# The scan's products of a pair of heads in three steps: by one direction's states, by the other's, by the inputs

## The chip, the cores and the metric

The kernel runs on one core of a Trainium2 chip, in one launch. The metric is the device time of the launch in microseconds (us). An execution under the hardware profiler gives the timelines quoted here.

## The reference

One layer of a diffusion backbone over 1024 latent tokens and 256 context tokens, width 1024: attention beside a bidirectional state-space scan, merged by gates, then a mixture of experts. The change is in the scan alone. Per direction it is a chunked recurrence:

```python
def ssd_chunked(xh, dt, a, bm, cm, h0, with_output):
    ...
    acum = jnp.cumsum(dtc * a, axis=2)
    ...
    cb = jnp.einsum('bcign,bcjgn->bcijg', cc, bc)
    y_diag = jnp.einsum('bcijg,bcijgr,bcjgr,bcjgrp->bcigrp', cb, decay, dtc, xc)
    y_off = jnp.einsum('bcign,cbgrpn,bcigr->bcigrp', cc, h_prev, jnp.exp(acum))
    y = (y_diag + y_off).reshape(nb, nl, ng, nr, npd)
```

There are 16 heads of 64 columns in 4 groups (a group shares B and C, of 128 states each). The output of a chunk is a sum of three products: the inputs of the chunk by a decayed matrix C B^T (`y_diag`, both directions in one matrix here), and C with the decay, by the forward state and by the backward state that come into the chunk (`y_off`, twice).

## The kernel before, in words

All of the layer's mixers run as coroutines of one planner, the class `Flow`. Each coroutine yields what it needs next: tiles, a free buffer of a ring, an engine, a time. The planner keeps a modelled clock for each engine and a modelled ready time for each tile. It resumes the coroutine that it thinks can go first, by priority, and the instructions are written into the engines' queues in that order. So the order on each engine is fixed when the program is built, and changing what a coroutine waits for can move instructions elsewhere. On the chip each engine runs its own queue in order, and semaphores hold an instruction until its operands are there.

The stage that matters is `mixer_t`. A server coroutine (the lowest priority) runs the in-projection: 24 multiplies of 512 columns for each bank (`acc`, four banks of PSUM; `hi`, `lo` are the split weights, `hh`, `hl` the split input). Its results go to the convolution (`conv_post`: ACT writes `ux`, `uB` or `uC` from the bank, then DVE adds two shifted copies per bank, after which the bank is free), or to gates. When the four convolutions of a group are there, `group` starts: it transposes the inputs (`xn`) and B (`Bn`), starts `states` once per direction (`hp[0]`, `hp[1]`: the states that enter each of the eight chunks of 128 tokens), multiplies C by B (`CB`, through the banks `aux`), and goes through four blocks: two pairs of heads by two halves of four chunks.

For each block and head, `unit` makes the operands. Two loads bring the cumulated decays, `R[0]` and `R[1]` (SP's queue, six buffers). DVE writes `W` by eight steps from the step sizes. POOL subtracts a column from `R[0]` into `G`, DVE's four steps combine it with `R[1]`, ACT takes the exponential. POOL multiplies W by CB, and DVE multiplies W by G: the matrix for the inputs. In `decays`, ACT takes the exponential of each R and POOL multiplies it by C: the matrices for the states. There are two buffers each of `W` and `G`.

`products` then runs 24 products of 128 columns into one bank `py`: for each of the four chunks W by xn, R[0] by hp[0], R[1] by hp[1], each for both heads, which take the two halves of the bank's partitions. It waits until both heads are listed in `ready`, and until 400 ns past the modelled ready times of their W and R. Afterwards the buffers go back, and `evac` adds the skip term and the gate on DVE. After four blocks `norm` ends the group.

Lines: L148 is every matmul, L156 activations, L171 and L175 two-tensor operations on DVE and POOL, L180 and L187 DVE operations with a column.

Of the kernel before, what the change touches and what calls it, by code (L numbers as in the profile page):

```python
# [19 lines left out]
P = 128  # L20
# [54 lines left out]
def _n(ap):  # L75
    return ap.tensor.name
# [299 lines left out]
class Layer:  # L376
# [413 lines left out]
    def mixer_t(s):  # L790
        tc, nc, I, F = s.tc, s.nc, s.I, s.F
# [9 lines left out]
        if True:  # L801
            acc = s.ring(pp, [P, 512], "acc", 4)
            aux = s.ring(pq, [P, 512], "aux", 2)
            pys = s.ring(pq, [P, 512], "py", 2)
# [11 lines left out]
            Rs = s.ring(sp, [P, 512], "R", 6)  # L816
            Gs = s.ring(sp, [P, 4, P], "G", 2)
            Ws = s.ring(sp, [P, 4, P], "W", 2)
# [172 lines left out]
            def group(g, x0, x1, B, C):  # L991
                x = (x0, x1)
                yield [lambda: state["dt"], xns, Bns]
                xn, Bn = xns.get(), Bns.get()
# [10 lines left out]
                for c in range(0, 10, 4):  # L1005
                    n = min(4, 10 - c)
# [8 lines left out]
                hp = [q.get() for q in hps]  # L1015
                done, left = [], [16]
# [4 lines left out]
                for half in range(2):  # L1021
                    yield [C, B, aux]
                    pt = aux.get()
                    for i in range(4):
                        c = 2 + half * 4 + i
# [6 lines left out]
                for pair in range(2):  # L1032
                    for half in range(2):
                        yield [pys]
                        py, ready = pys.get(), []
                        for hh in range(2):
                            yield [(Rs, 2), "NOW"]
                            F.spawn(0, unit(g, pair, half, hh, CB, C, ready))
                        F.spawn(1, products(g, pair, half, xn, hp, py, done, ready, yt))
# [39 lines left out]
            def unit(g, pair, half, hh, CB, C, ready):  # L1079

                r = 2 * pair + hh
                h = 4 * g + r
                t0 = 512 * half
                R = [Rs.get(), Rs.get()]
                for d in range(2):
                    F.dma(R[d], bass.AP(tensor=s.acd[d].tensor, offset=s.acd[d].offset + h * T + t0, ap=[[0, P], [1, 512]]))
                Rv = [q.rearrange("p (c i) -> p c i", i=P) for q in R]
                yield [Gs, Ws, "DVE"]
                G, W = Gs.get(), Ws.get()
                cs = range(4 * half, 4 * half + 4)  # L1090
                for c in range(4):
                    F.ts(W[:, c], s.le, dt[:, 2 + cs[c], h:h + 1], None, ALU.mult)
                for c in range(4):
                    F.stt(W[:, c], s.ge, dt[:, 2 + cs[c], 16 + h:16 + h + 1], W[:, c], ALU.mult, ALU.add)
                yield [R[0], "POOL"]
                F.ptt(G, Rv[0], ac[:, 0, 2 + 4 * half:6 + 4 * half, h:h + 1].to_broadcast([P, 4, P]), ALU.subtract)
                yield [G, R[1], "DVE"]
                for c in range(4):
                    F.stt(G[:, c], Rv[1][:, c], ac[:, 1, 2 + cs[c], h:h + 1], G[:, c], ALU.subtract, ALU.min)
                k = []  # L1100
                F.spawn(0, decays(R, C[:, t0:t0 + 512], k, F.clk["DVE"] + 100.0))
                yield [CB, W, "POOL"]
                F.ptt(W, W, CB[:, 4 * half:4 * half + 4], ALU.mult)
                yield [G, "ACT"]
                F.act(G, G, AF.Exp)
                yield [G, "DVE"]
                F.tt(W, W, G, ALU.mult)
                Gs.put(G)
                yield [lambda: len(k) == 2]
                ready.append((hh, W, *R))  # L1110

            def products(g, pair, half, xn, hp, py, done, ready, yt):

                yield [lambda: len(done) == 2 and len(ready) == 2]
                yield [hp[0], hp[1], *(F.ready[_n(q)] + 400.0 for v in ready for q in v[1:])]
                for c in range(4):
                    n = 4 * half + c
                    for i, src in enumerate((xn[:, 2 + n], hp[0][:, n], hp[1][:, n])):
                        for v in ready:
                            o = 64 * v[0]  # L1120
                            x = 128 * pair + o
                            F.mm(py[o:o + 64, c * P:(c + 1) * P], src[:, x:x + 64], v[1 + i].rearrange("p c i -> p (c i)")[:, c * P:(c + 1) * P] if i == 0 else v[1 + i][:, c * P:(c + 1) * P], i == 0, i == 2, 134.5)
                for _, W, R0, R1 in ready:
                    Rs.put(R0, R1)
                    Ws.put(W)
                yield from evac(g, pair, half, py, yt)

            def decays(R, C, k, at):
                for q in R:
                    yield [q, at, "ACT"]  # L1130
                    F.act(q, q, AF.Exp)
                    yield [q, "POOL"]
                    F.ptt(q, q, C, ALU.mult)
                    k.append(1)

            def evac(g, pair, half, py, yt):
                sl = slice(512 * half, 512 * half + 512)
# [1346 lines left out]
```

## Time and profile before

| what | us |
|---|---|
| median of 3 runs | 2785.7 (2785.47 to 2786.71) |
| the profiled execution | 2800.41 |
| its span | 2798.6 |
| PE busy in the span | 2618.5 |
| DVE busy in the span | 2013.0 |
| ACT, POOL busy in the span | 1340.7, 903.0 |

PE is TensorE's matmuls, DVE is VectorE, ACT is ScalarE, POOL is GpSimd, SP the queue that issues loads. A timeline row has the start, the duration, the engine, the line, the operation, out<-in, partitions by elements, and a count where equal instructions stand in sequence. Brackets at its end hold the idle time of the engine just before it, and what ended it. Durations of matmuls overlap: the distance of two starts tells what one costs. The scan's blocks run from about 500 to 1005 us; the four groups follow one another. A waits row counts idle time of one engine by what released it.

### The profile page before, as it was taken

The page shows a single profiled execution, that of the slowest core. Times are in us where ns is not written, and L with a number is a line of the kernel's source. Part 1 is how long each engine was busy: PE and PEld are TensorE (multiplying, and loading weights), DVE is VectorE, ACT ScalarE, POOL GpSimd, SP SyncE. Part 2 cuts the span into 40 slices and gives each one's busy share as a digit, 9 for nine tenths or more (in the row PEclk, how much of TensorE's full clock was granted, in tenths as well). Part 3 has the DMA queues.
Part 4 walks back from the last instruction along what each step waited for, and adds up shares of the span by engine and source line. Part 5 has one row for each costly group of instructions (what it writes and reads, how often), then busy time and mean ns, then how long its engine had stood idle before and what let it go on. Part 6 is the DMA issues. An engine that isn't in the chain of part 4 may idle for free.

```text
span 2798.6 us, 41131 instructions
## 1 busy us (share of the span) xinstructions
PE 2618.5 (94%) x14561; PEld 2101.1 (75%) x14561; DVE 2013.0 (72%) x4680; ACT 1340.7 (48%) x2104; POOL 903.0 (32%) x669
## 2 busy tenths in 40 slices
PE   7999999999999999999999999889999999999991
PEld 4888878778788777888887687668887776777660
DVE  6877133768686749888894767867788877788863
ACT  4211123344443546666664422435666656676651
POOL 0111010545353520000000000055656656677841
PEclk9999999999999999999999999999999999999996
DMA  7767253242334354223233953568899998999997
GB/s 277 224 206 216 64 143 105 67 139 91 121 91 132 106 172 145 82 91 141 93 102 125 292 179 133 188 216 264 276 309 297 315 299 278 307 321 328 314 316 233
DMA packets 275409, 545.67 MB, mean 195 GB/s; under 512 B 31562, under 2 KB 166835, under 8 KB 248194
## 3 DMA queue, kind: packets, MB, share of 16 engines
q1 hardware_dynamic: 239330, 437.14, 45.6%
q0 software_dynamic: 35872, 105.88, 14.8%
q8 instruction: 115, 1.88, 0.3%
q14 instruction: 92, 0.75, 0.1%
HBM read 433.78 MB, written 124.73 MB: 200 GB/s over the span
## 4 chain that ended last, share of the span: by engine, by line
PE 58%; DMA 10%; DVE 9%; issue 4%; ACT 2%; POOL 2%; SPq 0%; POOLq 0%; ACTq 0%; DVEq 0%
PE gu L148 16%; PE acc L148 10%; PE dn L148 9%; PE bacc L148 5%; PE sps L148 5%; PE pv L148 4%; DMA cr<-cumd,crow 3%; PE xt L152 2%; PE tr L152 2%; PE aux L148 2%; DVE G L187 2%; DMA qk<-qk 2%; DMA braw<-in_w_branch_attn_dram 1%; DVE gl L171 1%; DVE W L180 1%
## 5 line engine op out<-in xcount | busy, mean ns | idle before, releaser
L171 DVE TENSOR_TENSOR gl<-raw,gh 128x1024 fp32r<-128x1024 f32 x240 | 288.2, 1218 | 35.4 <-ACT gh L164 33.7
L148 PE MATMUL acc<-hh,hi 128*128 128x512 f32 (+2 forms) x760 | 304.7, 401 | 1.3 <-DVE ux L187 1.3
L148 PE MATMUL acc<-hl,hi 128*128 128x512 f32 (+2 forms) x760 | 289.3, 381 | 0.0
L164 ACT CAST gh<-raw 128x1024 fp32r<-128x1024 f32 x240 | 246.6, 1050 | 88.0 <-PE gu L148 59.2
L148 PE MATMUL acc<-hh,lo 128*128 128x512 f32 (+1 forms) x736 | 280.9, 382 | 2.5 <-DVE lo L171 2.5
L148 PE MATMUL gu<-gh,xh 128*128 128x512 f32 (+3 forms) x672 | 278.4, 414 | 0.6 <-ACT gh L164 0.6
L148 PE MATMUL gu<-gl,xh 128*128 128x512 f32 (+3 forms) x672 | 264.5, 394 | 6.2 <-DVE gl L171 4.4
L148 PE MATMUL gu<-gh,xl 128*128 128x512 f32 (+3 forms) x672 | 264.5, 394 | 0.0
L193 DVE TENSOR_SCALAR_CACHE_REDUCE e<-sps 128x512 f32<-128x512 f32 (+1 forms) x384 | 214.4, 597 | 32.9 <-PE sps L148 32.6
L262 POOL DMA_INDIRECT cr<-cumd,crow x98 | 123.4, 1260 | 316.1 <-DMA wtab<-sc 281.2
L268 POOL DMA_INDIRECT yacc<-y,tk x98 | 181.3, 1850 | 96.8 <-issue 23.2
L148 PE MATMUL sps<-qk 128*128 128x512 f32 (+1 forms) x768 | 195.6, 386 | 9.3 <-DMA qk<-qk 5.1
L156 ACT ACTIVATE e<-e,st 128x1280 f32<-128x1280 f32 x128 | 174.7, 1366 | 32.0 <-DVE st L202 31.8
L262 POOL DMA_INDIRECT wc<-wtab,tk x98 | 148.6, 1516 | 121.0 <-DVE tk L182 85.9
L148 PE MATMUL acc<-hi,hh 128*128 128x512 f32 x448 | 181.3, 405 | 0.0
L148 PE MATMUL acc<-hi,hl 128*128 128x512 f32 x448 | 176.2, 393 | 0.4 <-DVE hl L171 0.4
L148 PE MATMUL acc<-lo,hh 128*128 128x512 f32 x448 | 176.0, 393 | 0.0
L148 PEld LDWEIGHTS sps<-qk 128*128 128x128 f32 x768 | 141.2, 192 | 41.3 <-DVE e L193 8.3
L148 PEld LDWEIGHTS acc<-hh,hi 128*128 128x128 f32 (+1 forms) x760 | 142.6, 188 | 32.9 <-issue 4.0
L148 PE MATMUL pv<-wr,vv 128*128 128x256 f32 x640 | 165.1, 381 | 0.0
L148 PEld LDWEIGHTS acc<-hl,hi 128*128 128x128 f32 (+1 forms) x760 | 142.6, 188 | 27.4 <-issue 0.8
L148 PEld LDWEIGHTS acc<-hh,lo 128*128 128x128 f32 x736 | 138.7, 188 | 32.1 <-DVE lo L171 3.3
(327 smaller groups left out, 6264.3 us busy)
## 6 DMA issues: line engine op xcount, KB each, us to landing
raw<-in_w_e_gate_dram SPq DMA_DIRECT2D x64, 1024.0 KB
raw<-in_w_e_up_dram SPq DMA_DIRECT2D x64, 1024.0 KB
draw<-in_w_e_down_dram SPq DMA_DIRECT2D x64, 1024.0 KB
qk<-qk POOLq DMA_DIRECT2D x16, 1664.0 KB
raw<-in_w_in_dram SPq DMA_DIRECT2D x40, 512.0 KB
wada<-in_w_ada_dram SPq DMA_DIRECT2D x32, 512.0 KB
R<-acd SPq DMA_DIRECT2D x64, 256.0 KB
qk<-sa SPq DMA_DIRECT2D x52, 256.0 KB
```

The costliest lines, as they stand in the source:

```text
L148: s.nc.tensor.matmul(out, l, r, start=start, stop=stop)
L152: s.nc.tensor.transpose(out, in_, ident)
L156: s.nc.scalar.activation(out, in_, fn, **kw)
L164: s.nc.scalar.copy(out, in_)
L171: s.nc.vector.tensor_tensor(out, a, b, op=op)
L180: s.nc.vector.tensor_scalar(out, a, s1, s2, op0=op0)
L187: s.nc.vector.scalar_tensor_tensor(out, a, sc, b, op0=op0, op1=op1)
L193: s.nc.vector.tensor_scalar(out, a, s1, None, op0=op0, op1=op1, accum_out=acc)
L262: s.nc.gpsimd.indirect_dma_start(out=out, out_offset=None, in_=table, in_offset=bass.IndirectOffsetOnAxis(ap=idx, axis=0), **kw)
L268: s.nc.gpsimd.indirect_dma_start(out=table, out_offset=bass.IndirectOffsetOnAxis(ap=idx, axis=0), in_=in_, in_offset=None, compute_op=ALU. ...
```

## The change

`products` makes three steps instead of one loop over chunks. First R[0] by hp[0] for all four chunks and both heads, then R[1] by hp[1], then W by xn. Each step waits for its own operands, until 600 ns past the modelled ready time in the first two steps and 1000 ns in the last. `ready` becomes two lists: `decays` adds the R of a head to the first, `unit` adds its W to the second, and no longer waits for its `decays`. The R buffers go back after the second step, the W buffers after the third. The bank's start flag is set on the first chunk of the first step only, its stop flag on the last chunk of the last.

```diff
--- before.py
+++ after.py
@@ -1032,7 +1032,7 @@
                 for pair in range(2):
                     for half in range(2):
                         yield [pys]
-                        py, ready = pys.get(), []
+                        py, ready = pys.get(), ([], [])
                         for hh in range(2):
                             yield [(Rs, 2), "NOW"]
                             F.spawn(0, unit(g, pair, half, hh, CB, C, ready))
@@ -1097,8 +1097,7 @@
                 yield [G, R[1], "DVE"]
                 for c in range(4):
                     F.stt(G[:, c], Rv[1][:, c], ac[:, 1, 2 + cs[c], h:h + 1], G[:, c], ALU.subtract, ALU.min)
-                k = []
-                F.spawn(0, decays(R, C[:, t0:t0 + 512], k, F.clk["DVE"] + 100.0))
+                F.spawn(0, decays(R, C[:, t0:t0 + 512], hh, ready[0], F.clk["DVE"] + 100.0))
                 yield [CB, W, "POOL"]
                 F.ptt(W, W, CB[:, 4 * half:4 * half + 4], ALU.mult)
                 yield [G, "ACT"]
@@ -1106,32 +1105,40 @@
                 yield [G, "DVE"]
                 F.tt(W, W, G, ALU.mult)
                 Gs.put(G)
-                yield [lambda: len(k) == 2]
-                ready.append((hh, W, *R))
+                ready[1].append((hh, W))
 
             def products(g, pair, half, xn, hp, py, done, ready, yt):
 
-                yield [lambda: len(done) == 2 and len(ready) == 2]
-                yield [hp[0], hp[1], *(F.ready[_n(q)] + 400.0 for v in ready for q in v[1:])]
-                for c in range(4):
-                    n = 4 * half + c
-                    for i, src in enumerate((xn[:, 2 + n], hp[0][:, n], hp[1][:, n])):
-                        for v in ready:
-                            o = 64 * v[0]
+                yield [lambda: len(done) == 2 and len(ready[0]) == 2]
+
+                def part(srcs, ws, first, last):
+                    for c in range(4):
+                        for hh, w in ws:
+                            o = 64 * hh
                             x = 128 * pair + o
-                            F.mm(py[o:o + 64, c * P:(c + 1) * P], src[:, x:x + 64], v[1 + i].rearrange("p c i -> p (c i)")[:, c * P:(c + 1) * P] if i == 0 else v[1 + i][:, c * P:(c + 1) * P], i == 0, i == 2, 134.5)
-                for _, W, R0, R1 in ready:
-                    Rs.put(R0, R1)
-                    Ws.put(W)
+                            F.mm(py[o:o + 64, c * P:(c + 1) * P], srcs[c][:, x:x + 64], w[:, c * P:(c + 1) * P], first and c == 0, last and c == 3, 134.5)
+
+                ns = range(4 * half, 4 * half + 4)
+                for d in range(2):
+                    ws = [(v[0], v[1 + d]) for v in ready[0]]
+                    yield [hp[d], *(F.ready[_n(w)] + 600.0 for _, w in ws)]
+                    part([hp[d][:, n] for n in ns], ws, d == 0, False)
+                for v in ready[0]:
+                    Rs.put(*v[1:])
+                yield [lambda: len(ready[1]) == 2]
+                yield [xn, *(F.ready[_n(w)] + 1000.0 for _, w in ready[1])]
+                part([xn[:, 2 + n] for n in ns], [(hh, w.rearrange("p c i -> p (c i)")) for hh, w in ready[1]], False, True)
+                for _, w in ready[1]:
+                    Ws.put(w)
                 yield from evac(g, pair, half, py, yt)
 
-            def decays(R, C, k, at):
+            def decays(R, C, hh, ready, at):
                 for q in R:
                     yield [q, at, "ACT"]
                     F.act(q, q, AF.Exp)
                     yield [q, "POOL"]
                     F.ptt(q, q, C, ALU.mult)
-                    k.append(1)
+                ready.append((hh, *R))
 
             def evac(g, pair, half, py, yt):
                 sl = slice(512 * half, 512 * half + 512)
```

Each engine has the same instructions as before but for three fewer table loads on ACT. Up to the first block, and again from the first products of the branches that follow the scan, the orders are equal. The first place is PE at the fourth block of the first group; `hp_3824` and `hp_3825` are the forward and the backward states. Before (the pattern of the last rows goes on to 24 products):

```order
L148 MATMUL acc<-hh_85,hi 128x512
L148 MATMUL acc<-hl_86,hi 128x512
L148 MATMUL acc<-hh_85,lo 128x512
L148 MATMUL py<-W,xn 64x128 x2
L148 MATMUL py<-R,hp_3824 64x128 x2
L148 MATMUL py<-R,hp_3825 64x128 x2
L148 MATMUL py<-W,xn 64x128 x2
L148 MATMUL py<-R,hp_3824 64x128 x2
L148 MATMUL py<-R,hp_3825 64x128 x2
```

Now:

```order
L148 MATMUL acc<-hh_83,lo 128x512
L148 MATMUL py<-R,hp_3824 64x128 x8
L148 MATMUL acc<-hh_83,hi 128x512
L148 MATMUL acc<-hl_84,hi 128x512
L148 MATMUL acc<-hh_83,lo 128x512
L148 MATMUL acc<-hh_83,hi 128x512
L148 MATMUL acc<-hl_84,hi 128x512
L148 MATMUL acc<-hh_83,lo 128x512
L148 MATMUL py<-R,hp_3825 64x128 x8
L148 MATMUL py<-W,xn 64x128 x8
L148 MATMUL acc<-hh_85,hi 128x512
L148 MATMUL acc<-hl_86,hi 128x512
```

The block comes after 9 fewer accumulations, and six stand between its first two steps. This is one of four such blocks; in the other twelve the steps stand back to back.

The second place is DVE at the start of the second group's blocks, where the states' last steps (hp) meet the first block's W and G. Before:

```order
L187 SCALAR_TENSOR_TENSOR hp_4988<-hp_4988,cdec,aux 128x64 x12
L187 SCALAR_TENSOR_TENSOR ux<-acc,vcol,ux 128x512
L187 SCALAR_TENSOR_TENSOR ux<-acc,vcol,ux 128x511 x2
L187 SCALAR_TENSOR_TENSOR ux<-acc,vcol,ux 128x512
L187 SCALAR_TENSOR_TENSOR ux<-acc,vcol,ux 128x255 x2
L171 TENSOR_TENSOR lo<-raw,hi 128x512
L180 TENSOR_SCALAR W<-cst,dtn 128x128 x4
L187 SCALAR_TENSOR_TENSOR W<-cst,dtn,W 128x128 x4
L180 TENSOR_SCALAR W<-cst,dtn 128x128 x4
L187 SCALAR_TENSOR_TENSOR W<-cst,dtn,W 128x128 x4
L187 SCALAR_TENSOR_TENSOR G<-R,ac,G 128x128 x8
L171 TENSOR_TENSOR W<-W,G 128x512
```

Now (the planner has given the states of the same direction the name `hp_4995`):

```order
L187 SCALAR_TENSOR_TENSOR hp_4995<-hp_4995,cdec,aux 128x64 x8
L180 TENSOR_SCALAR W<-cst,dtn 128x128 x4
L187 SCALAR_TENSOR_TENSOR W<-cst,dtn,W 128x128 x4
L187 SCALAR_TENSOR_TENSOR hp_4995<-hp_4995,cdec,aux 128x64 x4
L180 TENSOR_SCALAR W<-cst,dtn 128x128 x4
L187 SCALAR_TENSOR_TENSOR W<-cst,dtn,W 128x128 x4
L187 SCALAR_TENSOR_TENSOR hp_4995<-hp_4995,cdec,aux 128x64 x4
L187 SCALAR_TENSOR_TENSOR G<-R,ac,G 128x128 x8
L171 TENSOR_TENSOR W<-W,G 128x512
L187 SCALAR_TENSOR_TENSOR ux<-acc,vcol,ux 128x512
L171 TENSOR_TENSOR W<-W,G 128x512
L187 SCALAR_TENSOR_TENSOR ux<-acc,vcol,ux 128x511
```

Both heads' W now stand ahead of the last steps of the states, and the convolution's steps (ux) behind the first multiply of W by G. In the first group it was like this before already.

The third place is PE just ahead of the second group's first block, now, with the semaphores that an instruction waits for (`DVE_49`, `Pool_49` are counters of DVE and of POOL):

```order
L148 MATMUL acc<-hl_84,hi 128x512
L148 MATMUL acc<-hh_83,lo 128x512
L148 MATMUL acc<-hh_85,hi 128x512 [waits DVE_49]
L148 MATMUL acc<-hl_86,hi 128x512
L148 MATMUL acc<-hh_85,lo 128x512
L148 MATMUL acc<-hh_85,hi 128x512
L148 MATMUL acc<-hl_86,hi 128x512
L148 MATMUL acc<-hh_85,lo 128x512
L148 MATMUL acc<-hh_85,hi 128x512
L148 MATMUL acc<-hl_86,hi 128x512
L148 MATMUL acc<-hh_85,lo 128x512
L148 MATMUL py<-R,hp_4994 64x128 [waits Pool_49] x2
```

The accumulation into a fresh bank waits for a step of DVE, which is `ux<-acc` of the rows above; eight more and the block stand behind it. The third group has the same.

## Rows read from the trace of the kernel before

**Rows 1.** The page's first line.

```profile
span 2798.6 us, 41131 instructions
```

**Rows 2.** Busy time by engine, clock, DMA share, in two stretches of the scan.

```profile
500.00:1005.00 505.00, 479.23 (x2798) 395.92 (x2797) 370.92 (x874) 229.36 (x326) 239.67 (x198) 0.99 0.36 108
...
680.00:720.00 40.00, 36.77 (x236) 29.74 (x235) 37.98 (x67) 19.61 (x28) 25.56 (x20) 1.00 0.38 120
```

**Rows 3.** PE's waits, 500 to 1010: in total, times, longest.

```profile
PE py L148 <- DVE W L171: 14.5, 8, 2.6
...
PE py L148 <- POOL R L175: 7.3, 9, 3.3
```

**Rows 4.** The chain, 495 to 515: start, us, what.

```profile
507.93 2.09 PE acc L148 x9
```

**Rows 5.** PE's timeline, first group: start, us, instruction, [idle before it, its releaser].

```profile
521.28 0.58 PE L148 MATMUL acc<-hh,hi 128*128 128x512 f32 x1
...
532.76 0.50 PE L148 MATMUL acc<-hh,hi 128*128 128x512 f32 x1 [1.30 <-DVE ux L187]
...
535.07 0.44 PE L148 MATMUL py<-W,xn 128*64 128x128 f32 x4
...
537.84 0.50 PE L148 MATMUL acc<-hh,hi 128*128 128x512 f32 x1
...
553.34 0.32 PE L148 MATMUL py<-R,hp 128*64 128x128 f32 x1 [0.48 <-POOL R L175]
...
572.97 0.32 PE L148 MATMUL py<-R,hp 128*64 128x128 f32 x1 [0.47 <-POOL R L175]
...
591.82 0.32 PE L148 MATMUL py<-R,hp 128*64 128x128 f32 x1 [0.47 <-POOL R L175]
...
595.67 0.61 PE L148 MATMUL acc<-hh,hi 128*128 128x512 f32 x1
```

**Rows 6.** DVE's timeline, first group.

```profile
522.44 0.87 DVE L180 TENSOR_SCALAR W<-cst,dtn 128x128 f32<-128x128 f32 x4
...
524.28 2.19 DVE L187 SCALAR_TENSOR_TENSOR G<-R,ac,G 128x128 f32<-128x128 f32 x8
...
539.34 1.14 DVE L187 SCALAR_TENSOR_TENSOR G<-R,ac,G 128x128 f32<-128x128 f32 x4
...
583.85 5.27 DVE L187 SCALAR_TENSOR_TENSOR G<-R,ac,G 128x128 f32<-128x128 f32 x4 [0.95 <-POOL G L175]
```

**Rows 7.** PE's timeline, second group.

```profile
648.39 0.47 PE L148 MATMUL acc<-hh,hi 128*128 128x256 f32 x1
...
649.29 1.05 PE L148 MATMUL aux<-uC,uB 128*128 128x128 f32 x8
...
725.80 0.47 PE L148 MATMUL py<-W,xn 128*64 128x128 f32 x1 [2.64 <-DVE W L171]
...
730.13 0.50 PE L148 MATMUL acc<-hh,hi 128*128 128x512 f32 x1
```

**Rows 8.** POOL's timeline, first group.

```profile
528.50 6.38 POOL L175 TENSOR_TENSOR R<-R,uC 128x512 f32<-128x512 f32 x4 [0.88 <-ACT R L156]
...
582.49 1.33 POOL L175 TENSOR_TENSOR G<-R,ac 128x512 f32<-128x512 f32 x1 [1.91 <-DMA R<-acd]
```

**Rows 9.** PE's timeline, third group.

```profile
782.75 0.47 PE L148 MATMUL acc<-hh,hi 128*128 128x256 f32 x1
...
859.84 0.32 PE L148 MATMUL py<-W,xn 128*64 128x128 f32 x1 [0.62 <-DVE W L171]
...
862.61 0.50 PE L148 MATMUL acc<-hh,hi 128*128 128x512 f32 x1
```

**Rows 10.** Busy time and clock around the wait in the second group.

```profile
725.00:730.00 5.00, 4.20 (x46) 4.15 (x46) 2.55 (x4) 3.59 (x6) 1.46 (x2) 0.66 0.28 53
```

**Rows 11.** PE's timeline, end of the scan.

```profile
1004.92 1.05 PE L148 MATMUL aux<-cst,G 128*128 128x1 f32 x8 [0.40 <-POOL G L175]
...
1032.12 0.50 PE L148 MATMUL bacc<-bxh,bwh 128*128 128x512 f32 x1 [0.47 <-ACT bxh L164]
```

## The prediction

> **What bounds the kernel now.** I read the page's totals first, then the stretch in which the scan runs, then TensorE's waits there, then the timelines of single blocks. The profiled execution took 2800.41 us for a span of 2798.6 [rows 1]; the sum below is made against it, and since the runs shown have a median of 2785.7 (2785.47 to 2786.71), 0.53% less, the result is scaled by 2785.7 / 2800.41 = 0.99475. In the scan, 500 to 1005 us, PE is busy for 479.23 of 505 us [rows 2]: so all that any order of the products can win there is about 26 us, 0.9% of the kernel. The table of PE's waits names them: 14.5 us in 8 waits of a product for DVE's last multiply of W, 7.3 us in 9 waits for POOL's multiply of R [rows 3]. The reader is to see that these waits are not spread: between two product blocks PE has accumulations of the in-projection (0.233 us each, 9 in 2.09) [rows 4] until they run out, and then it stands. What it stands for is the chain of the next pair's operands on DVE, POOL and ACT. In 680 to 720, DVE is busy for 37.98 of 40 us [rows 2]. So the scan has two engines close to full, and a stretch is as long as the longer of them: PE's work placed there, or DVE's chain of blocks.
>
> **What the change does to PE's order.** The products stay the same 24 per block, 2.77 us from the first to the next accumulation (535.07 to 537.84) [rows 5]. Of 16 blocks, 12 have their three steps without anything between; only four have six accumulations (6 x 0.233 = 1.4 us) between the first step and the second. So the change of order inside a block moves little by itself. What it moves is where the planner puts whole blocks. From the planned order I count PE's work between the last state product and the end of the fourth block. In the second and third group it falls by 66 accumulations of 512 columns (66 x 0.233 = 15.4), six of 256 (half of that each, 0.7) and the eight products C by B (649.29 to 650.10 on PE's clock, about 0.8 for four and four beside each other, so 2 x 0.8 = 1.6) [rows 7]: 17.7 us in each of the two groups. In the first group it falls by nine accumulations, 2.1 us; in the fourth it is equal. This work does not go away: it stands before the states or after the scan, where the order now has 96 more accumulations ahead of the branches' first products. There it costs its own time. So a group gains only if its block chain gets shorter by more than the work taken out of it.
>
> **The first group, as a measure of the chain.** Its start in the new order is the same as now, and the new second and third groups are ordered like it: W of the first block is set before the last states are done. From the accumulation behind the last state product (521.28) to the end of block 1 (537.84) are 16.56 us [rows 5]. Then the last operand, each time a POOL multiply of R, came at 553.34, 572.97 and 591.82 [rows 5]: 15.50 us after the end of block 1, then 19.63 and 18.85.
>
> **The second and third group after.** *Block 1.* PE could end it 8.6 us after the anchor if nothing were late (25 accumulations, 5.8, and 2.77 for the block): the lower bound. The upper bound is the first group's 16.56. Of that, one set of W, 1.84 us (522.44 to 524.28) [rows 6], now stands ahead of the states' last steps, and POOL's idle 0.88 us before its four multiplies of R [rows 8], which was ACT's late first exponential, should go. 16.56 - 1.84 - 0.88 = 13.8. I take it, because those multiplies ended at 534.88 (528.50 + 6.38) and the products began at 535.07: the row that the block hangs on. The added wait belongs here: in the new order the nine accumulations just ahead of block 1 need a bank that DVE's convolution step (ux<-acc) empties, and that stands behind the multiply of W by G of the first head. The first group has the pattern already: 1.30 us at 532.76 [rows 5]. Behind that accumulation stand the other eight and then block 1 itself. It is inside the 13.8.
> *The steps.* R comes free after the second step, eight products (0.92 us, a third of 2.77) before the block's end. The two later blocks each had a first POOL subtraction waiting for the load of R (1.91 at 582.49) [rows 8], so I take 0.92 off the two later intervals: 18.71 and 17.93. Lower bound for an interval: 15.50, the shortest seen; upper: as before. When R lands last, the first eight products have run, and 16 remain: 1.85 us.
> *The clock.* After a wait the fourth block of the second group ran its 22 last products in 4.33 us (725.80 to 730.13) instead of 2.54, with a granted clock of 0.66 as a mean over 725 to 730 [rows 7, 10], so part of it at the lower of the two levels, 1.2 GHz: 1.8 us lost. The first group's lost 1.4 (its last 18 products took 3.85 from 591.82, against 2.4 with the first rows of a block). The third's lost none. I leave it so.
> *Sum.* Second: 13.8 + 15.5 + 18.7 + 17.9 + 1.85 + 1.8 = 69.6, plus 17.7 done elsewhere = 87.3, against 81.74 now (648.39 to 730.13) [rows 7]: +5.5. Third: 67.8 + 17.7 = 85.5 against 79.86 (782.75 to 862.61) [rows 9]: +5.6. First: last operand at 70.54, less 2 x 0.92, then 1.85 and 1.4, is 71.95; plus 2.1 elsewhere, against 74.39: -0.3. Fourth: same work between its blocks, other places: 0, within 3 on both sides. Tail: PE's waits of 0.40 and 0.47 before the branches [rows 11] are covered by the 96 accumulations: -0.9. Total +9.9; 2810.3 x 0.99475 = 2795.5. I forecast 2795.
>
> **A rule weighed.** DVE's four steps of G took 5.27 us from 583.85, when POOL multiplied at the same time, and 1.14 from 539.34, when it did not [rows 6]. The Trainium skill ("SBUF — State Buffer", Who interferes with whom) states that VectorE and GpSimd share one pair of ports as an exclusive lock; so an instruction that needs it waits the other out. The two rows agree with this. By the slow row the chain of a block stays as long as I have it; by the fast one each of three blocks of three groups could lose up to 4.1 us, if the new order kept POOL out of those steps. I see nothing in the order that does, and it is what separates my forecast from rival D.
>
> **Rivals.**
> *B, no change.* Block 1 of the second and third group comes when PE's order has it, at 8.6 instead of 13.8, since its W is set early and R's loads have long landed: 2 x -5.2 = -10.4 on the sum, so -0.5, and 2785. For it: W's own multiplies and G are before the states' end in DVE's order. Against it: POOL's row of 6.38 us for four multiplies.
> *C, slower still, by the clock.* Waits of 2 us and more appear before more blocks, since PE has 15 us of work for each instead of 16. If two more blocks in each of three groups run at the lower level, 6 x 1.8 = +10.8, 2806. It decides from the third wait of over 2 us in a group. For it: 725.80 after a wait of 2.64. Against: 859.84 after one of 0.62 stayed at full clock [rows 9]. The Trainium skill ("TensorE: Matmul & The Clock Gate", HAM oscillation) describes such recurring gaps as what lowers the clock each time; here the rows show it after some waits only.
> *D, faster.* The chain per block is no longer than the first interval, 15.50, in all groups, because R is free early and the G steps run beside less of POOL. Second: 13.8 + 46.5 + 1.85 + 17.7 = 79.85, -1.9; third 0.0; first 16.56 + 46.5 + 1.85 + 2.1 = 67.0, -7.4; tail -0.9. Sum -10.2, 2775. For it: PE's work between blocks is now 14 to 15 us, so such a chain would leave almost no wait. Against it: DVE is at 95% between blocks now.
> *E, nothing.* That the steps do not matter, being adjacent in 12 of 16 blocks, is true of the order inside a block but not of the blocks' places; I count it under B.
>
> **How the numbers follow.** Forecast 0.40, B 0.27, C 0.12, D 0.21. The forecast's own range is 2790 to 2801: no half clock at all takes 3.2 off, no gain from R's earlier return adds 5.5, block 1 a little earlier takes 2 more. A measurement can tell 0.2%, 5.6 us, so faster is under 2780 and slower over 2791. D and a little of B make 0.24 faster, the rest of B and the low end of the forecast 0.28 same, the rest and C 0.48 slower. The range reaches from D to C, 2774 to 2806; beyond it lie all the intervals short with block 1 early, and all long with a lowered clock.
>
> **What would show it.** In the profile after, PE's waits between 500 and 1010 us should have grown to about 35 us, most of them for POOL's R in front of the second step, and few for W. The second group should take about 70 us from its last state product to the end of block 4. Waits under 20 us there would say D; block 1 within 9 us of the last state product would say B; a granted clock well under 0.99 over 500 to 1005 would say C. The forecast is wrong if the chain of operands is not what the blocks wait for: then the wait is elsewhere, or the work moved out of the scan was covering other waits there.

## The result and the profile after

The changed kernel takes 2801.9 us (median of 6 runs, 2799.75 to 2813.2), the kernel before 2786.12 in the same runs: a ratio of 1.0066, interval 1.0047 to 1.0085: slower by 16 us by the medians, by 18 by the ratio. The forecast was 2795, slower, with a range of 2774 to 2806.

The two profiled executions are almost equal in span, 2798.6 and 2799.3. That comes from behind the scan, where the profiled execution of before lost time that no later profile shows: from the first transposes of the branches to its end it took 1722.9 us, the changed kernel 1703.2, the twelve kernels of the experiments 1704.4 to 1713.5. So the scan is read by itself. These are the first transposes, before and after, in PE's timeline:

```profile
1075.74 0.41 PE L152 MATMUL tr<-cst,e 128*128 128x128 f32 x1
```

```profile
1096.10 0.41 PE L152 MATMUL tr<-cst,e 128*128 128x128 f32 x1
```

20.4 us later, with the same work ahead. The scan's last block ends at the same time in both. These are the accumulations behind it, before and after:

```profile
996.55 0.50 PE L148 MATMUL acc<-hh,hi 128*128 128x512 f32 x1
```

```profile
996.63 0.50 PE L148 MATMUL acc<-hh,hi 128*128 128x512 f32 x1
```

But in the planned order 270 accumulations instead of 183 stand between that block and the transposes, and 87 x 0.233 is 20.3 us (the prediction has 96 more). So the groups and what lies between them took as long as before with 87 accumulations less in them, and the rest of this section is on what filled the place. PE's waits between 500 and 1010 us after (what was waited for, us in total, times, longest) answer to [rows 3]:

```profile
PE py L148 <- POOL R L175: 24.1, 13, 2.5
PE acc L148 <- DVE ux L187: 11.9, 3, 5.3
PE acc L148 <- DVE lo L171: 1.5, 1, 1.5
PE aux L148 <- POOL G L175: 0.7, 2, 0.5
```

They sum to 38.2 us; before, with the smaller groups (1.9 for lo, 1.3 for ux, 0.7 for G), to 25.7. No wait is for W any more, which now comes last in a block. The waits of products grew by only 2.3 us; 10.6 of the 12.5 are accumulations waiting for a bank. Of the 24.1 for R, 16.3 stand in front of the second step and 7.7 in front of the first. The second loss is in the clock (the first of the three numbers at a row's end). Answering to [rows 2]:

```profile
500.00:1005.00 505.00, 466.76 (x2721) 384.08 (x2720) 377.74 (x873) 221.10 (x316) 230.69 (x200) 0.97 0.35 104
```

Summed over stretches of 5 us from 500 to 1040, five times (1 - clock), the lowered clock takes 6.8 us before and 15.4 after: +8.6. With the waits this is 21.1, but some 2.2 of it are counted twice, since PE stood idle for 4.6 us of the lowered stretches (0.2 before). So 19 of the 20.4 are accounted for. This is the second group on PE, answering to [rows 7]:

```profile
655.12 0.58 PE L148 MATMUL acc<-hh,hi 128*128 128x512 f32 x1
...
664.28 0.80 PE L148 MATMUL acc<-hh,hi 128*128 128x512 f32 x1 [5.32 <-DVE ux L187]
...
668.06 0.33 PE L148 MATMUL py<-R,hp 128*64 128x128 f32 x2
...
670.83 0.50 PE L148 MATMUL acc<-hh,hi 128*128 128x512 f32 x1
...
686.78 0.33 PE L148 MATMUL py<-R,hp 128*64 128x128 f32 x2 [2.51 <-POOL R L175]
...
706.48 0.33 PE L148 MATMUL py<-R,hp 128*64 128x128 f32 x2 [2.11 <-POOL R L175]
...
722.43 0.48 PE L148 MATMUL py<-R,hp 128*64 128x128 f32 x2 [2.24 <-POOL R L175]
...
728.38 0.50 PE L148 MATMUL acc<-hh,hi 128*128 128x512 f32 x1
```

From the last state product to the end of block 4 it takes 73.26 us instead of 81.74, but it holds 17.7 us less of PE's work. The third group does the same (787.85 to 859.95: 72.1 against 79.86 [rows 9]). Behind the 5.32 the accumulations run at the lower level: their starts are 0.43 us apart instead of 0.23. Of 795 to 800, where the same wait ends in the third group, the row is

```profile
795.00:800.00 5.00, 2.98 (x7) 2.43 (x8) 4.99 (x7) 2.06 (x4) 3.90 (x3) 0.50 0.00 0
```

PE is busy for 2.98 of these 5.00 us: the lower level was granted while it still waited.

Why the bank is late, and what block 1 hangs on, stands in three engines' timelines of the second group. DVE:

```profile
657.91 3.69 DVE L187 SCALAR_TENSOR_TENSOR G<-R,ac,G 128x128 f32<-128x128 f32 x8
661.52 0.68 DVE L171 TENSOR_TENSOR W<-W,G 128x512 f32<-128x512 f32 x1
662.12 0.74 DVE L187 SCALAR_TENSOR_TENSOR ux<-acc,vcol,ux 128x512 f32<-128x512 f32 x1
662.87 0.69 DVE L171 TENSOR_TENSOR W<-W,G 128x512 f32<-128x512 f32 x1
663.48 0.74 DVE L187 SCALAR_TENSOR_TENSOR ux<-acc,vcol,ux 128x511 f32<-128x511 f32 x1
```

ACT, and POOL:

```profile
660.58 0.63 ACT L156 ACTIVATE G<-G 128x512 f32<-128x512 f32 x1 [5.10 <-DVE G L187]
661.12 1.12 ACT L164 CAST hi<-raw 128x512 fp32r<-128x512 f32 x2
662.14 0.62 ACT L156 ACTIVATE G<-G 128x512 f32<-128x512 f32 x1
662.67 1.65 ACT L156 ACTIVATE R<-R 128x512 f32<-128x512 f32 x3
```

```profile
663.36 4.71 POOL L175 TENSOR_TENSOR R<-R,uC 128x512 f32<-128x512 f32 x3 [3.49 <-ACT R L156]
```

ACT had written ux from the bank by 652.7; of DVE's two steps for it, one stands behind the first head's multiply of W by G and the other behind the second's; that one ends at 664.2, which releases the accumulation. POOL waits 3.49 us for three of the four R: on ACT they stand behind two exponentials of G and two casts, and ACT itself waited 5.10 us there for DVE's steps of G. POOL's multiplies of R end at 668.07, just when the products begin: two late things side by side.

### The profile page after: what moved, and what is told of

Read it like the earlier page. It is cut to its first block, busy times and chain, and to the rows that moved or that the text cites. A ratio compares the mean times of both kernels' runs of the same rounds, so it can differ in the third digit from the quotient of the medians.

```text
span 2799.3 us, 41107 instructions
## 1 busy us (share of the span) xinstructions
PE 2616.7 (93%) x14561; PEld 2098.6 (75%) x14561; DVE 2021.8 (72%) x4680; ACT 1334.0 (48%) x2101; POOL 891.6 (32%) x669
## 3 DMA queue, kind: packets, MB, share of 16 engines
q0 software_dynamic: 35872, 105.88, 14.7%
## 4 chain that ended last, share of the span: by engine, by line
PE 43%; DMA 11%; DVE 6%; issue 3%; ACT 1%; POOL 1%; SPq 0%; POOLq 0%; ACTq 0%; DVEq 0%
PE gu L148 13%; PE dn L148 8%; PE bacc L148 6%; PE sps L148 5%; PE pv L148 4%; DMA cr<-cumd,crow 4%; PE tr L152 2%; DMA raw<-in_w_e_up_dram 2%; PE xt L152 2%; PE acc L148 2%; DMA qk<-qk 2%; DMA yacc<-y,tk 1%; DVE gl L171 1%; DMA z<-yacc 1%; PE hT L152 1%
## 6 DMA issues: line engine op xcount, KB each, us to landing
raw<-in_w_e_gate_dram SPq DMA_DIRECT2D x64, 1024.0 KB, 10.3
```

## The experiments

Where a kernel's name stands in a table below, "length" is the sum over the four groups of the time from the last state product to the end of block 4 in its profile, "work" what PE's planned order holds there at the rows' rates (0.233 for an accumulation, half for 256 columns, 0.1154 for a product, 0.2 for a product of C by B), and "loss" their difference. Kernels "in chunks" have the old order with its one wait.

**The new order behind the old wait.** In the kernel before:

```diff
-                for c in range(4):
...
-                    for i, src in enumerate((xn[:, 2 + n], hp[0][:, n], hp[1][:, n])):
+                for i in (1, 2, 0):
+                    for c in range(4):
+                        n = 4 * half + c
+                        src = (xn[:, 2 + n], hp[0][:, n], hp[1][:, n])[i]
...
```

> The kernel before with one edit: its 24 products of a block come in the new order of steps, but still behind the one old wait (both heads' W and R, 400 ns past their modelled times). Its planned order again puts the blocks of the second and third group early: PE's work from the last state product to the end of block 4 is 58 us there (before 72, changed kernel 54). Theory P (where the planner puts the blocks costs the time, not the split wait): 8 to 20 us slower than before, with waits of accumulations for ux in the second and third group. Rival S (the split waits, their slacks and the early R do it): within 6 us of before.

1.0099 (1.0083 to 1.0116), 2810.97 us: slower even than the changed kernel. Waits:

```profile
PE acc L148 <- DVE ux L187: 23.7, 6, 5.3
PE acc L148 <- DVE uB L187: 9.8, 3, 3.3
PE py L148 <- POOL R L175: 6.4, 8, 1.8
```

Rival S falls: this order loses without the split waits too, by 27 us over before, which is more than theory P's 8 to 20. With one wait the planner again puts blocks early, and 33.5 us go to banks.

**Blocks only after the states.** In the changed kernel:

```diff
-                        yield [pys]
+                        yield [pys, lambda: len(done) == 2]
```

> The changed kernel, but a group's blocks start only when both directions' states are done, so that no W of block 1 stands ahead of the last state steps on DVE. Theory U (the added wait of accumulations for ux, 11.9 us in the changed kernel, is half of the loss): that wait is under 3 us, and the time is 8 to 12 us less than the changed kernel's, so 4 to 12 us over before. Rival K (the chain of operands alone sets a group's length): the time moves by under 4 us against the changed kernel, the wait for ux comes back as waits of products.

1.0048 (1.0031 to 1.0065), 2798.84: about 5 us under the changed kernel's ratio, between the two theories, and the two intervals overlap. The wait for ux falls to 2.2 us, the clock takes 8.5 instead of 15.4; but waits for lo rise from 1.5 to 5.6 and the blocks' R is as late as ever:

```profile
PE py L148 <- POOL R L175: 23.4, 18, 2.7
```

**Less of POOL's multiply.** In the changed kernel, the planned order kept; the multiply by C is left out for three of the four chunks, so this is a measure and not a kernel to use:

```diff
-                    F.ptt(q, q, C, ALU.mult)
+                    nc.gpsimd.tensor_tensor(q[:, :P], q[:, :P], C[:, :P], op=ALU.mult)
+                    F.op("POOL", 36 + 2.22 * 512, q, (q, C))
```

> The changed kernel; POOL multiplies only the first 128 of 512 columns of each R by C (the other columns stay without C), the order is the same. Theory R (blocks wait for POOL's multiplies of R, and POOL slows DVE's G steps when it runs beside them): PE's waits for R fall from 24 us to under 8, the mean of DVE's G steps falls from about 670 ns to under 500, and the time falls by 15 us or more. Rival D (DVE's own list is the bound): the waits change their name to W and stay over 15 us, the time falls by under 6 us.

0.9942 (0.9928 to 0.9956), 2769.29: 33 us under the changed kernel. PE's waits for R (L1140 is the shortened multiply):

```profile
PE py L148 <- POOL R L1140: 4.5, 6, 1.5
```

DVE's G steps fall from a mean of 690 ns to 548. In the groups' table (line, engine, operation, count | busy, mean ns | idle), the changed kernel and this one:

```profile
L187 DVE SCALAR_TENSOR_TENSOR G<-R,ac,G 128x128 f32<-128x128 f32 x128 | 80.5, 690 | 0.0
```

```profile
L187 DVE SCALAR_TENSOR_TENSOR G<-R,ac,G 128x128 f32<-128x128 f32 x128 | 62.4, 548 | 0.0
```

Theory R holds in its waits and its time, though the mean stayed above 500: in the same order, a shorter multiply on POOL makes the groups shorter by 33 us. Rival D's sign, waits for W over 15 us, is not there: there are none. But DVE's steps got faster too, so the run does not part POOL's own time from what it costs DVE.

**The waits filled.** In the changed kernel, blocks 2 and 3:

```diff
                     part([hp[d][:, n] for n in ns], ws, d == 0, False)
+                    if d == 0 and pair + half == 1:
+                        for i in range(16):
+                            hh, q = ready[0][i % 2][:2]
+                            c = i // 2 % 4
+                            nc.tensor.matmul(py[64 * hh:64 * hh + 64, c * P:(c + 1) * P], zz, q[:, c * P:(c + 1) * P], start=False, stop=False)
```

> The changed kernel with 16 products by a tile of zeros (1.83 us of PE's work) between the first and the second step of blocks 2 and 3 of each group, where PE waits for R. Theory H (the waits are real and let the clock fall; the lowered clock costs about 8 us more than in the kernel before): the time is the same or up to 7 us less than the changed kernel's, with fewer stretches at the lower level behind blocks 2 and 3. Rival W (PE is not idle there in the runs without the profiler, or the clock falls for other reasons): 8 x 1.83, up to 14 us slower.

1.0094 (1.0076 to 1.0111), 2812.95: about 8 us slower than the changed kernel, for 14.6 us of added work. By the time alone it is inconclusive, since 8 us also lies in rival W's range. Counted from the last state product, in the first three groups blocks 2 and 3 end no more than 0.7 us later in spite of the fill: PE was idle there. But the fourth block of each ends 0.7 to 3.0 later, and that of the fourth group 3.5. Behind blocks 2 and 3 the clock no longer falls, but it does ahead of or in block 4 of the first three groups and for longer in the second group's wait for a bank, so that it took 13.75 us, hardly less. Whether a kept clock pays is not shown.

**The convolution first.** In the changed kernel:

```diff
-                    F.spawn(0, conv_post(q, v, 0 if q >= 12 else L, banks))
+                    F.spawn(-1, conv_post(q, v, 0 if q >= 12 else L, banks))
```

> The changed kernel, but the coroutine that finishes a convolution goes ahead of the blocks' operands wherever both are ready (priority -1 instead of 0). Theory U (banks held by convolution steps that stand behind the blocks' W steps on DVE cost about 10 us directly, and lower the clock): waits for ux under 3 us, time 6 to 14 us under the changed kernel. Rival K (operands' chain sets the length, the wait only moves): PE's waits for R grow by what the others lose, time within 4 us of the changed kernel.

1.006 (1.0041 to 1.0078), 2801.21: no gain, as rival K has it, but not for K's reason. There is no wait for ux, the clock takes 3.4 us, R's waits even fall to 21.3; the loss in the four groups is 38.7 us against 61.3. What was won goes behind the scan:

```profile
1066.94 0.80 PE L148 MATMUL bacc<-bxh,bwh 128*128 128x512 f32 x1 [7.51 <-ACT bwh L164]
```

That is a branch's product waiting for its weights while the DMA engines are full (in 1060 to 1070 their share is 1.05, at 363 GB/s):

```profile
1060.00:1070.00 10.00, 3.06 (x7) 2.44 (x8) 1.80 (x6) 3.11 (x3) 0.00 (x0) 0.70 1.05 363
```

The last block ends 13 us later in PE's order than before, so 13 us fewer accumulations are left to stand over the loads. From the last block to the first transposes it takes 83.2 us, before 79.2 with that much more work: PE is idle for 17.1 us of it (5.4 before), and the lowered clock takes 11.3 (4.4 before).

**Less slack.** In the changed kernel 600, 600 and 1000 become 400:

```diff
-                    yield [hp[d], *(F.ready[_n(w)] + 600.0 for _, w in ws)]
+                    yield [hp[d], *(F.ready[_n(w)] + 400.0 for _, w in ws)]
...
-                yield [xn, *(F.ready[_n(w)] + 1000.0 for _, w in ready[1])]
+                yield [xn, *(F.ready[_n(w)] + 400.0 for _, w in ready[1])]
```

> The changed kernel with 400 ns past the modelled times in all three steps, instead of 600, 600 and 1000. The planner then puts the second group's blocks late (block 1 ends after 22.4 us of PE's work, third group 19.6), as in the kernel before. Theory P (early blocks in the second and third group are the loss): no wait for ux over 2 us, time within 8 us of the kernel before. Rival S (the larger slacks protect; less slack means longer waits): waits for W and R grow by 16 x 0.2 to 0.6 us, time like the changed kernel's or above.

1.0103 (1.0084 to 1.0123), 2814.82. Late blocks with hardly a wait for ux (1.9 us in two), and still the slowest of the three-step kernels. So theory P, as I put it, is wrong: it isn't the early start as such. As rival S has it, the waits for R grew and the time lies above the changed kernel's.

```profile
PE py L148 <- POOL R L175: 31.9, 19, 3.4
```

The clock takes 23.9 us.

**Part of DVE's work to ACT**, in the changed kernel and in the one before:

```diff
-                yield [Gs, Ws, "DVE"]
+                yield [Gs, Ws, "ACT"]
...
-                    F.ts(W[:, c], s.le, dt[:, 2 + cs[c], h:h + 1], None, ALU.mult)
+                    F.act(W[:, c], s.le, AF.Identity, scale=dt[:, 2 + cs[c], h:h + 1])
+                yield [W, "DVE"]
```

> The changed kernel, but the first four steps of each W (a mask by a step size) run on ACT instead of DVE: 47.7 us of DVE's 371 between 500 and 1005 in the kernel before. Blocks of groups 2 and 3 come late here (23.4 us of PE's work to the end of block 1). Theory D (DVE's list, stretched by POOL, is the chain): PE's waits in the scan fall from 38 to under 20 us, and the time is under the kernel before by 5 to 20 us. Rival R (POOL's list is the chain): waits for R stay over 18 us, time within 6 us of the kernel before or above.

> The kernel before (chunk by chunk, one wait) with the same edit: W's first four steps on ACT. Here the planner puts the blocks of groups 2 and 3 early (block 1 ends after 12.5 us of PE's work). Theory P (early blocks cost, whatever the order of the products): waits of accumulations for ux over 10 us, and at least 8 us slower than the changed kernel with the same edit. Rival S (the three steps cost): at least 5 us faster than the changed kernel with the same edit.

The first: 1.0014 (1.0002 to 1.0026), 2788.87; R's waits 20.8 us, so rival R: with DVE's own list shortened most of them stayed. The second: 1.0189 (1.0166 to 1.0212), 2835.48, 47 us slower than the first, from banks and clock (30.8 us), with early blocks and one wait:

```profile
PE acc L148 <- DVE ux L187: 24.6, 6, 5.6
PE py L148 <- POOL R L175: 15.9, 8, 3.4
PE acc L148 <- DVE uB L187: 7.3, 3, 2.8
```

Its blocks stand early and lose at the banks, as theory P has it; the three steps, with their blocks late, win. That the place and not the steps made the difference is a sign only: both differ between the two.

**POOL's subtraction to ACT as well.** On the changed kernel with the edit above (`dtd` holds the negated decays by then):

```diff
-                yield [R[0], "POOL"]
-                F.ptt(G, Rv[0], ac[:, 0, 2 + 4 * half:6 + 4 * half, h:h + 1].to_broadcast([P, 4, P]), ALU.subtract)
+                yield [R[0], "ACT"]
+                for c in range(4):
+                    F.act(G[:, c], Rv[0][:, c], AF.Identity, bias=dtd[:, 2 + cs[c], h:h + 1])
```

> The changed kernel with two shares of the operands' work on ACT: W's first four steps (from DVE) and the subtraction into G (from POOL, 32 instructions of 1.04 to 1.9 us). Blocks of groups 2 and 3 end block 1 after 20.7 us of PE's work. Theory R (POOL's list, which also stretches DVE's steps, is the chain behind the waits): waits for R under 12 us, DVE's G steps under 700 ns in the mean, and 8 to 20 us less than the kernel before. Rival A (the chain goes through ACT or through the buffers of W, which come free only at a block's end): within 6 us of the kernel before, waits for R or W over 18 us.

Then the same with the convolution first, and the kernel before with this edit alone:

> The same, and the convolution's coroutine goes ahead of the blocks' operands. Theory R: as the one without it or up to 8 us less, no wait for ux. Theory T (what is won in the scan is given back behind it, where the branches' weights arrive no sooner): the scan's blocks end earlier but the first transposes of the branches come no earlier than 78 us after the last block; time within 4 us of the one without it.

> The kernel before (chunk by chunk, one wait) with the subtraction into G on ACT instead of POOL, nothing else. Blocks of groups 2 and 3 stand late, as in the kernel before (23.4 and 22.4 us of PE's work to the end of block 1). Theory R: PE's waits in the scan fall from 25.7 to under 16 us, 5 to 15 us less than the kernel before. Rival A: within 5 us of it or slower.

The first: 1.001 (1.0 to 1.0019), 2788.57. Waits for R fall to 5.7 and the G steps to a mean of 455 ns, as theory R has it, but the time, put at 8 to 20 us under before, is 3 us above it: the waits go to banks (ux 13.1, uB 5.0). With the convolution first:

```profile
PE py L148 <- POOL R L175: 19.0, 18, 4.0
PE acc L148 <- DVE lo L171: 0.8, 1, 0.8
```

0.9978 (0.9968 to 0.9988), 2777.12 us: faster than both kernels by their ratios, and 9 to 11 us from the convolution's place alone, more than either theory allows. The waits at the banks are gone, and most of them came back as waits for R. Its first transposes come 78.5 us after the last block, but that is no bound of the loads: the planned order leaves as much work there as the kernel before does, and a kernel with less (the next) took 75.2. The third is a miss for theory R, and rival A's case: 1.0079 (1.0065 to 1.0093), 2804.97, with 24.1 us of waits for W, the longest 5.6. Why W is late there is not followed up.

**The best kernel without the steps.** Last, the kernel before with all three edits:

> The kernel before (chunk by chunk, one wait) with all three edits of the best kernel so far: W's first steps and the subtraction into G on ACT, and the convolution's coroutine ahead of the blocks' operands. Between the two stands only the order of the products with its waits. Theory P (the three steps as such cost nothing; what costs is where blocks and convolution steps stand): within 6 us of the kernel with three steps, 2771 to 2783. Theory S+ (the three steps let the products by the states run while W is still being made, and so win): 8 us or more slower than it, waits for W over 15 us. Theory S- (the three steps cost): 8 us or more faster than it.

1.0037 (1.0023 to 1.0051), 2794.84, against 0.9978 with three steps: both signs of theory S+. Its waits are

```profile
PE py L148 <- DVE W L171: 15.8, 6, 4.4
PE py L148 <- POOL R L175: 7.0, 10, 1.5
PE acc L148 <- DVE lo L171: 0.6, 2, 0.3
```

but in all they are only 3.6 us more than with three steps, where those for R are longer. The larger part is the clock, 18.7 us against 6.9. So the 16 us belong to the two whole orders; that they come from W being out of the way is not shown.

The account over all of these but the fill, whose added work is not the kernel's (the last column is the ratio's distance from 1, times 2785):

| kernel | length | work | loss | loss against before | measured |
|---|---|---|---|---|---|
| before | 315.7 | 272.7 | 43.0 | | |
| changed | 294.4 | 233.0 | 61.3 | +18.3 | +18.4 |
| order, old wait | 315.7 | 247.0 | 68.7 | +25.7 | +27.6 |
| after the states | 314.9 | 259.6 | 55.3 | +12.3 | +13.4 |
| short multiply | 261.3 | 233.0 | 28.3 | -14.7 | -16.2 |
| slack 400 | 320.3 | 249.9 | 70.4 | +27.4 | +28.7 |
| W on ACT, three steps | 310.4 | 266.4 | 44.0 | +1.0 | +3.9 |
| W on ACT, chunks | 337.7 | 249.8 | 87.8 | +44.8 | +52.6 |
| both on ACT | 299.6 | 257.9 | 41.7 | -1.3 | +2.8 |
| and convolution first | 294.9 | 256.9 | 38.0 | -5.0 | -6.1 |
| G on ACT, chunks | 319.9 | 265.3 | 54.6 | +11.6 | +22.0 |
| all three edits, chunks | 315.4 | 265.3 | 50.1 | +7.1 | +10.3 |
| convolution first | 301.9 | 263.2 | 38.7 | -4.3 | +16.7 |

Length follows work only in part: the changed kernel has 39.7 us less of it than before and is 21.3 shorter, the old wait in the new order has 25.7 less and is no shorter at all. With work the same, the short multiply alone takes 33 us off the length: so in that order the chain of operands sets it, and what the planner doesn't put into it is lost. The table says where the time goes, not why. Nine of the twelve rows agree within 5 us. Two of the kernels in chunks are off by 7.8 and 10.4, not followed up, and the last row is off by 21.0, for what lies behind the scan.

## Why the prediction was right, and what it missed

**The direction and the mechanism** were right: PE's work taken out of the second and third group (17.7 us each) was not matched by shorter chains. Waits were put at about 35 us, mostly for R, few for W: 38.2, 24.1 and none. The run that shortened POOL's multiply shows the chain at work: with PE's order the same, the time fell by 33 us. The size was less sure: 2801.9 lies just above the forecast's own 2790 to 2801, and in the stated range because that reaches to rival C.

**The sum was too small**: +9.9 of the scan's 20.4. Its terms were mis-sized so:

- *Block 1*, 13.8 us: measured 15.71 and 15.90 in the two groups. The step that failed is "POOL's idle 0.88 us should go". It became 3.49, since ACT's order has two casts and two exponentials of G, for the first of which it waited 5.10, ahead of the other three R. I had read DVE's order and PE's, not ACT's. (This is read from the timelines; no run moved ACT's order alone.) The wait for ux was 5.32, not the 1.30 of the first group, but it is a second late thing beside R, which was ready no sooner. What the block would take without it is not shown: with the convolution first it took 17.08, but there 16.7 us of PE's work stand up to its end, instead of 8.3.
- *The interval after block 2*, 18.71, with R's loads 0.92 earlier: measured 19.70 and 19.59. R's early return gave nothing there; the first interval came as put, 15.95 against 15.50.
- *The last interval and what follows it*: in the second group the interval was 15.95 instead of 17.93, but from the last operand to the end of block 4 it took 5.95, not 1.85 and 1.8. The sum has R late in front of the second step; the row at 722.43 is in the first, so nearly all products and the six accumulations stood behind it, part of them at the lower clock. The two errors nearly cancel, which is luck. In the third group the two terms together were 20.66 against 19.78.
- *The clock* was left as it was, and took 8.6 us more. Part of that fell in waits, so it cost some 6. Rival C's mechanism was at work, behind waits of products as it said and behind those for ux, which it did not name; its sign, a third wait of over 2 us, is in the second and the third group, and the clock over 500 to 1005 is 0.97. It was a rival with a chance of 0.12, and should have been a term of the sum. The trace of before had more of it than the prediction read, which looked at fourth blocks alone: in block 3 of the third and of the fourth group the clock was lowered too (from 841.67 and from 974.79).
- *First group*: -0.3 forecast, +0.9 measured (73.19 and 2.1 against 74.39). *Fourth*: 0 forecast, -1.7. Its work isn't equal, as the prediction has it: six accumulations and four products of C by B fewer, 2.2 us, and it got 3.9 shorter. *Tail*: -0.9 forecast; the waits before the branches (0.40 and 0.47) became 0.2 and 0.60, no gain.

**Rival D** (chain as short as 15.50 in all groups) did not come true: the second interval stayed above 19 us. The G steps took 690 ns in the mean in the changed kernel, 548 with POOL's multiply cut, and 455 with POOL's subtraction and W's first steps on ACT. That is the direction of the rule in the Trainium skill ("SBUF — State Buffer", Who interferes with whom), that VectorE and GpSimd share a pair of ports as an exclusive lock. It does not come out in every order: with the subtraction alone on ACT, in chunks, the mean was 648 against 670 before. And the fast row of 1.14 us at 539.34 was read wrongly: the prediction has it without POOL, but POOL multiplied beside it, and there it was POOL that took long (such a multiply took 1.29 at 657.30 in the changed kernel):

```profile
539.57 2.13 POOL L175 TENSOR_TENSOR W<-W,CB 128x512 f32<-128x512 f32 x1 [3.23 <-DVE W L187]
```

**Rival E**, that the steps don't matter by themselves, is not borne out. Alike in the other edits they are worth 0.0037 + 0.0022 of 2785, 16 us. With one wait in the new order the kernel was 9 us slower than with the three. But each such pair differs in where blocks stand as well, so what the steps are worth in one place is not shown.

**Not settled**: why slack 400 leaves R so late with late blocks, what the wait for a bank costs by itself, and how much of the clock's 8.6 us one could keep. "After the states" took 6.9 off the clock's share and won about 5; the fill took off 1.7, and its added work hides what that won.

## What to carry to other kernels

Where a planner orders several engines, an edit inside one stage is first a change of the place of everything around it: count the filler work in each stretch of the new order and set it against the chain's length in the profile, for every engine of the chain, before costing the edit itself. Work moved out of a stretch whose length a chain sets comes back elsewhere (here 20.3 us behind the scan), and work moved into it may be missed where later loads need a cover. So check the next stage's cover before counting a gain in a stage. And read the order of every engine that the chain passes through, not of the two busiest.

## What the runs showed of the hardware

DVE's first steps of W, which read one tile and a column, are stretched as much beside POOL as the G steps that read two: four took 0.87 us at 670.93 in the changed kernel, and four 5.08 at 673.83, while POOL ran from 673.00 to 678.83 with hardly a gap:

```profile
670.93 0.87 DVE L180 TENSOR_SCALAR W<-cst,dtn 128x128 f32<-128x128 f32 x4 [2.43 <-PE py L148]
...
673.83 5.08 DVE L180 TENSOR_SCALAR W<-cst,dtn 128x128 f32<-128x128 f32 x4
```

The clock fell to its lower level in seven places of the changed kernel's scan and four of the kernel's before, in or behind waits. In the changed kernel it was lowered behind waits of 2.50 us (554.96) and 1.95 us (574.57), and stayed up behind 2.11 us (706.48) and 2.53 us (819.70): the length of one wait does not tell it.
